# The running sum of a depthwise convolution: in one PSUM bank instead of SBUF

## The chip, the core and the metric

The kernel runs on one core of one Trainium2 chip. The metric is the device time of one launch in microseconds (us); lower is better. A measurement of this kernel can tell a difference of about 0.2%.

The engines are named as in the profile: PE is TensorE (matmuls; PEld is its weight load), DVE is VectorE, ACT is ScalarE, POOL is GpSimd, and SP is SyncE, whose queue issues nearly all DMAs. L506 is line 506 of the kernel. SBUF is the on-chip memory that all engines reach. PSUM holds eight banks of 128 partitions x 512 float32 values; matmuls write there.

## The reference, cut to what matters

Two residual layers of width 1024 over 512 positions. Layer 0 mixes positions with a Fourier half and a convolution half of 512 channels each, layer 1 with windowed attention, and each is followed by a mixture of 16 experts. The change lies in the convolution half of layer 0:

```python
def fourier_conv_mixer(h, w_in, conv_w, conv_b, ln_g, ln_b, w_out):
    proj = h @ w_in
    u_f = proj[..., :FOURIER_WIDTH]
    u_v = proj[..., FOURIER_WIDTH:FOURIER_WIDTH + CONV_WIDTH]
    u_g = proj[..., FOURIER_WIDTH + CONV_WIDTH:]
    ...
    glu = u_v * jax.nn.sigmoid(u_g)
    pad = CONV_KERNEL // 2
    conv = lax.conv_general_dilated(
        glu, conv_w[:, None, :], window_strides=(1,), padding=[(pad, pad)],
        dimension_numbers=("NWC", "WIO", "NWC"), feature_group_count=CONV_WIDTH) + conv_b
    y_c = jax.nn.silu(layer_norm(conv, ln_g, ln_b))
    return jnp.concatenate([y_f, y_c], axis=-1) @ w_out
```

The convolution is depthwise: each channel is filtered by itself, with 31 taps, over all 512 positions.

## The kernel before, in words

**Layout.** Activations lie transposed: channels on the 128 partitions, the 512 positions along the free dimension. The 512 convolution channels are four tiles, ct 0 to 3.

**The convolution.** `gated(ct)` multiplies the normalised input by the value and gate columns of `w_in` (three matmuls in `mm3`, L141 to L143, for one product in split precision) into two PSUM banks. `glu_of` then takes the sigmoid on ACT (L515) and writes the product to `glu[ct]` in SBUF on DVE (L516); in the trace that tile is named 3a for ct 0 and 1 and 3b for ct 2 and 3. `conv(ct, split)` sums 31 shifted copies of `glu[ct]`, each times one number per channel, into `ym[4 + ct]` (named 0b, SBUF). For ct 0, 2 and 3 all of it is DVE's: one `tensor_scalar` (L498) and thirty `scalar_tensor_tensor` (L506), each of which reads the shifted input and the sum from SBUF and writes the sum to SBUF. For ct 1 the argument is 30: ACT makes each tap's product (L503) in one of two buffers in 4b, and POOL adds it to the sum (L504).

**What else runs in that stretch.** PE does the projections, the Fourier half (`fourier`, `spectrum`: L542 to L544 and L551, with POOL additions L534 to L537 before them) and products that make the conditioning vectors (`ada_block`: L227, then L287, whose PSUM result DVE reduces at L289 and L290). Another way to the same kind of vector is `ada_steps`: DVE multiplies and adds weight tiles from DMA (L268, L266), or ACT and POOL do (L262, L264). Weights that need split precision go through `halves`: ACT rounds (L118), POOL or DVE subtracts (L119). `y_parts` does the same for an activation tile (L565 on ACT, L566 on POOL or DVE).

**After it.** Token L of the list `toks` needs all four tiles: it sums over channels with PE (`sums`, L579), forms the mean (L649) and subtracts it on DVE (L651). Token M does the same with squares (L656, L660, L666), token N normalises (L670, L671). The output projection (`out_mm`, `add_gated` L395), the router (L740 to L800) and the first mixture of experts (`moe`: L920 gathers tokens, L976 multiplies them by expert weights) follow.

**What sets the order.** `toks` gives the order in which the program is written. A scheduler with a timeline model then reorders the instructions of each engine, and each engine runs its own list strictly in order, waiting on semaphores. PSUM banks come from `free_banks`, eight in all, handed out and given back in the order of the code. Weight buffers (`Slot`, 11 of 1 MB and some areas lent to them) are handed out the same way, so a DMA into one waits until the buffer's last reader is done.

Of the kernel before, what the change touches and what calls it, by code (L numbers as in the profile page):

```python
# [12 lines left out]
AF = mybir.ActivationFunctionType  # L13
OP = mybir.AluOpType
# [18 lines left out]
def trunk(ctx: ExitStack, tc: tile.TileContext, x_d, c_d, pos_d, ada_w, ada_b, mix_g, ffn_g, w_in,  # L33
# [366 lines left out]
    def mixer0():  # L400
# [89 lines left out]

        def conv(ct, split):

            cv, g = ym[4 + ct], glu[ct]
            wt = lambda k: cw[:, 4 * k + ct:4 * k + ct + 1]
            if split:
                nc.scalar.activation(cv, g[:, 0:S], AF.Identity, scale=wt(0), bias=colsC[:, 24 + ct:25 + ct])
            else:
                nc.vector.tensor_scalar(cv, g[:, 0:S], wt(0), colsC[:, 24 + ct:25 + ct],  # L498
                                        op0=OP.mult, op1=OP.add)
            for k in range(1, TAPS):  # L500
                if k <= split:
                    f = taps[k % 2]
                    nc.scalar.activation(f, g[:, k:k + S], AF.Copy, scale=wt(k))  # L503
                    nc.gpsimd.tensor_add(cv, cv, f)  # L504
                else:
                    nc.vector.scalar_tensor_tensor(cv, g[:, k:k + S], wt(k), cv, op0=OP.mult, op1=OP.add)  # L506

        todo = [(0, 0, 4), (0, 0, 5)] + [(0, 1, j) for j in range(4)]
        G0 = None
        bs = [Bank() for _ in range(6)]  # L510
        pss = [b.__enter__() for b in bs]
        tiles = [(w, P * j) for j in range(2) for w in w0] + [(wf0, P * j) for j in range(2)]
        def glu_of(ct, pg, pv):
            sg = tmp()
            nc.scalar.activation(sg, pg, AF.Sigmoid)  # L515
            nc.vector.tensor_mul(glu[ct][:, PAD:PAD + S], pv, sg)  # L516

        def gated(ct):
            if ct > 1:
                bs_ = [Bank(), Bank()]  # L520
                ps = [b.__enter__() for b in bs_]
            else:
                bs_, ps = bs[2 * ct:2 * ct + 2], pss[2 * ct:2 * ct + 2]
            for p, m in zip(ps, w1 if ct > 1 else w0):
                proj(p, m, P * (ct % 2), range(0 if ct > 1 else 4, KT))
            glu_of(ct, *ps)
            back_banks(bs_)

        def spectrum(g, u):
# [68 lines left out]
        for tok in toks:  # L598
# [16 lines left out]
            elif op == 'n':  # L615
                lent = lend()
            elif op == 'F':
                us[j] = fourier(j)
            elif op == 's':
                G0 = G0 or Slot()  # L620
                if not ym[0]:
                    ym[0:4] = fourths("0a")
                spectrum(j, us.pop(j))
            elif op in "DE" and arg in ("d", "p"):
                drip += ada_steps(*(todo if op == 'D' else more)[j], arg == "p")
                if op == 'E':
                    more[j] = None
            elif op == 'D':
                ada_block(*todo[j], "0a" if arg else None)
            elif op == 'E':  # L630
                ada_block(*more[j])
                more[j] = None
            elif op == 'P':
                free_slots[:0] = [free_slots.pop(min(i, len(free_slots) - 1)) for i in picks]
            elif op == 'w':
                wf1 = wcols(256)
            elif op == 'H':
                G0.back()
                hh, hl = h_area()
                yp = list(zip(hh, hl))  # L640
                free_slots.extend(areas[2:])
            elif op == 'y':
                y_parts(j, eng)
            elif op == 'O':
                wo[j // 2, j % 2] = wo_half(j // 2, j % 2, eng)
            elif op == 'L':
                f = sums([ym[4 + ct] for ct in range(4)])
                with Bank() as pm:
                    nc.tensor.matmul(pm, mean4, f, start=True, stop=True)  # L649
                    for ct in range(4):  # L650
                        nc.vector.tensor_sub(ym[4 + ct], ym[4 + ct], pm)  # L651
                prefix_matrices()
            elif op == 'M':
                sq = [g[:, 0:S] for g in glu]
                for ct in range(4):
                    nc.scalar.activation(sq[ct], ym[4 + ct], AF.Square)  # L656
                f = sums(sq)
                with Bank() as pq:
                    for t in range(TT):
                        nc.tensor.matmul(pq[:, t:t + 1], f[:, P * t:P * t + P], ind, start=True, stop=True)  # L660
                    nc.vector.tensor_scalar(va, pq[:, 0:TT], 512 * EPS, None, op0=OP.add)
                rsqrt(rs, va, TT, 512 ** 0.5)
                prb = Bank()
                pr = prb.__enter__()
                for t in range(TT):
                    nc.tensor.matmul(pr[:, P * t:P * t + P], rs[:, t:t + 1].to_broadcast([P, P]), ident,  # L666
                                     start=True, stop=True)
            elif op == 'N':
                y = ym[4 + j]
                nc.vector.tensor_mul(y, y, pr)  # L670
                nc.scalar.activation(y, y, AF.Silu, scale=colsC[:, 28 + j:29 + j], bias=colsC[:, 32 + j:33 + j])  # L671
                y_parts(4 + j, nc.gpsimd if arg == 'g' else nc.vector)
                if j == 3:
                    prb.__exit__()
            elif op == 'e':
                early[j] = Bank()
                early[j] = early[j], early[j].__enter__()
                out_mm(early[j][1], j % TT, j // TT, range(4))
            elif op == 'B':
                row_bcast(gbc, mod[0, 0][:, 16:24])  # L680
            elif op == 'G':
                unlend(lent)
                free_slots.extend(areas[:2])
            elif op == 'T':
                rt = Router(0)
            elif op == 'm':
                first = 4
                if j not in early:
                    early[j] = Bank()
                    early[j] = early[j], early[j].__enter__()  # L690
                    first = 0
                t, hf = j % TT, j // TT
                out_mm(early[j][1], t, hf, range(first, KT))
                add_gated(t, hf, early[j][1], {'v': nc.vector, 'g': nc.gpsimd, None: nc.vector if hf else nc.gpsimd}[arg])
                early[j][0].__exit__()
                left[hf] -= 1
                if left[hf] == 0:
                    for i in range(2):
                        back(wo.pop((hf, i)))
            elif op == 'r':  # L700
                flip[0] = int(arg) if arg else flip[0]
                rt.part(j % 4, j // 4)
            elif op == 'V':
                drip += rt.early()
# [783 lines left out]
```

## Time and profile before

| | |
|---|---|
| Median of three runs | 1507.4 us (1506.88 to 1508.84) |
| The profiled execution, its own time | 1508.68 us |
| Its span, first to last instruction | 1507.0 us |
| Busy share of the span: PE, DVE, ACT, POOL | 91%, 42%, 22%, 21% |
| DMA | 480.69 MB, 319 GB/s on average |
| Mean granted TensorE clock | 0.961 |

The profile is one execution, so all sums below are made against its own 1508.68 us; 1.68 us of that lie around the span. Busy shares are averages over stages that have different limits, so a stage is read by itself, from a table of windows. In a timeline row the first number is the start and the second the time from there to the end of the last instruction that is merged into the row; instructions of one engine may overlap slightly, so the pace of a series is the distance from start to start.

### The profile page before, as it was taken

What the parts mean: (1) busy time and instruction counts of PE and PEld (TensorE: products, weight loads), DVE (VectorE), ACT (ScalarE), POOL (GpSimd) and SP (SyncE); (2) the same over time, 40 slices, a digit from 0 to 9 for tenths busy, and PEclk for the clock granted to TensorE, in tenths of its full rate; (3) what the DMA queues carried; (4) which work ended last, traced back from release to release, by engine and by line L of the source; (5) the groups of instructions that cost most, each with busy time, mean ns of one, the idle gap of its engine ahead of it and who ended that gap; (6) DMA issues with size and microseconds to landing.
All of it is one profiled execution on the core that took longest, in us unless ns stands there. A gap on an engine that the chain in (4) does not pass through costs nothing.

```text
span 1507.0 us, 18064 instructions
## 1 busy us (share of the span) xinstructions
PE 1367.3 (91%) x7203; PEld 764.9 (51%) x7203; DVE 635.7 (42%) x1165; ACT 337.7 (22%) x686; POOL 312.0 (21%) x234
## 2 busy tenths in 40 slices
PE   5994699899999999999878989989999999999996
PEld 3673475555355353453457656645554454443433
DVE  5599956322222221122267888771222222222114
ACT  3353343110010010100246554421110010010002
POOL 2587741200000000000046563500000000000002
PEclk8997899899999999999989999989999999999998
DMA  9466379789999999999910365877899999999995
GB/s 329 127 217 214 121 278 381 298 340 398 402 411 410 411 410 411 411 410 410 366 33 28 107 200 169 279 283 280 329 412 400 410 410 411 410 411 410 411 406 204
DMA packets 158428, 480.69 MB, mean 319 GB/s; under 512 B 10416, under 2 KB 31176, under 8 KB 158344
## 3 DMA queue, kind: packets, MB, share of 16 engines
q1 hardware_dynamic: 158264, 479.27, 83.0%
q8 instruction: 57, 0.93, 0.3%
q0 software_dynamic: 80, 0.26, 0.0%
q14 instruction: 27, 0.22, 0.0%
HBM read 477.40 MB, written 2.10 MB: 318 GB/s over the span
## 4 chain that ended last, share of the span: by engine, by line
PE 62%; DVE 17%; DMA 16%; ACT 2%; issue 1%; SPq 1%; POOL 0%; DVEq 0%; ACTq 0%; POOLq 0%
PE bank L976 32%; PE bank L920 8%; DVE 0b L506 7%; DMA w<-in_moe_w_up_dram 6%; DMA w<-in_moe_w_gate_dram 5%; PE bank L141 3%; PE bank L142 3%; PE bank L143 3%; PE bank L997 3%; PE bank L1014 3%; DMA 4b<-in_moe_w_gate_dram 2%; PE bank L227 2%; DMA 4a<-in_moe_w_up_dram 1%; PE bank L1305 1%; DMA 4a<-in_fc_w_in_dram 1%
## 5 line engine op out<-in xcount | busy, mean ns | idle before, releaser
L976 PE MATMUL bank<-w,area2b 128*64 128x512 f32 x744 | 194.3, 595 | 9.4 <-DMA w<-in_moe_w_gate_dram 6.5
L976 PE MATMUL bank<-w,area1b 128*64 128x512 f32 x688 | 182.0, 595 | 7.1 <-DMA w<-in_moe_w_up_dram 4.3
L976 PE MATMUL bank<-w,area1a 128*64 128x512 f32 x624 | 158.0, 593 | 3.4 <-ACT area1a L153 2.2
L1017 DVE TENSOR_TENSOR x<-x,bank 128x512 f32<-128x512 f32 (+1 forms) x136 | 78.8, 649 | 187.5 <-PE bank L1014 187.5
L909 POOL TENSOR_TENSOR tmp<-tmp,rr 128x512 f32<-128x512 f32 x14 | 17.7, 1265 | 589.6 <-DVE tmp L903 567.8
L976 PEld LDWEIGHTS bank<-w,area2b 128*64 128x64 f32 x744 | 62.0, 137 | 109.1 <-issue 85.4
L1067 DVE TENSOR_TENSOR area1a<-bank,area1a 128x512 f32<-128x512 f32 x32 | 22.1, 692 | 219.1 <-PE bank L976 219.1
L1007 DVE SCALAR_TENSOR_TENSOR tmp<-bank,af,gbc 128x512 f32<-128x512 f32 (+1 forms) x34 | 24.5, 720 | 213.3 <-PE bank L976 185.1
L976 PEld LDWEIGHTS bank<-w,area1b 128*64 128x64 f32 x688 | 58.8, 137 | 106.6 <-issue 84.6
L119 POOL TENSOR_TENSOR w<-w,w 128x1024 fp32r<-128x1024 f32 x30 | 75.5, 2533 | 148.6 <-ACT w L118 142.5
L976 PEld LDWEIGHTS bank<-w,area1a 128*64 128x64 f32 x624 | 53.1, 137 | 77.5 <-issue 70.1
L506 DVE SCALAR_TENSOR_TENSOR 0b<-3b,cw,0b 128x512 f32<-128x512 f32 x60 | 69.0, 1185 | 0.1
L1014 PE MATMUL bank<-area2a 128*128 128x512 f32 (+1 forms) x272 | 64.2, 386 | 5.1 <-ACT area2a L1008 5.1
L1008 ACT ACTIVATE area2a<-tmp 128x512 fp32r<-128x512 f32 (+1 forms) x34 | 20.6, 607 | 214.3 <-DVE tmp L1007 214.3
L1043 ACT ACTIVATE area1a<-bank 128x512 f32<-128x512 f32 x32 | 19.2, 599 | 195.4 <-PE bank L976 195.4
L1014 PEld LDWEIGHTS bank<-area2a 128*128 128x128 f32 x272 | 47.9, 188 | 28.2 <-ACT area1a L1043 9.7
L920 PE MATMUL bank<-tmp,0a 128*128 128x128 f32 x384 | 59.8, 278 | 0.0
L141 PE MATMUL bank<-area1a,w 128*128 128x512 f32 x132 | 53.0, 421 | 7.4 <-ACT area1a L377 6.6
L920 PE MATMUL bank<-tmp,0b 128*128 128x128 f32 x384 | 58.6, 275 | 0.0
L926 ACT ACTIVATE area1b<-bank,mod,a 128x128 f32<-128x128 f32 x32 | 14.6, 457 | 184.3 <-DVE area1b L928 184.3
L920 PEld LDWEIGHTS bank<-tmp,0a 128*128 128x128 f32 x384 | 50.5, 192 | 9.7 <-issue 9.7
L143 PE MATMUL bank<-area1a,w 128*128 128x512 f32 x132 | 53.4, 406 | 1.2 <-POOL w L119 1.2
(466 smaller groups left out, 2673.3 us busy)
## 6 DMA issues: line engine op xcount, KB each, us to landing
w<-in_moe_w_gate_dram SPq DMA_DIRECT2D x93, 1024.0 KB, 18.1
w<-in_moe_w_up_dram SPq DMA_DIRECT2D x86, 1024.0 KB, 18.2
w<-in_moe_w_down_dram SPq DMA_DIRECT2D x85, 1024.0 KB, 18.2
w<-in_ada_w_dram SPq DMA_DIRECT2D x44, 1024.0 KB, 7.0
3b<-in_moe_w_up_dram SPq DMA_DIRECT2D x10, 1024.0 KB, 18.6
4b<-in_moe_w_gate_dram SPq DMA_DIRECT2D x9, 1024.0 KB, 18.4
4a<-in_moe_w_gate_dram SPq DMA_DIRECT2D x9, 1024.0 KB, 18.0
3a<-in_moe_w_up_dram SPq DMA_DIRECT2D x9, 1024.0 KB, 15.5
```

What stands on the lines that cost most here:

```text
L119: eng.tensor_sub(lo.ap[:, s], w.ap[:, s], hi.ap[:, s].bitcast(FT))
L141: nc.tensor.matmul(ps, l[0], r[0], start=start, stop=False)
L142: nc.tensor.matmul(ps, l[0], r[1], start=False, stop=False)
L143: nc.tensor.matmul(ps, l[1], r[0], start=False, stop=stop)
L227: nc.tensor.matmul(ps[32 * q:32 * q + 32], cond[:, 4 * half + q], w[:, q], start=half == 0, stop=half == 1)
L506: nc.vector.scalar_tensor_tensor(cv, g[:, k:k + S], wt(k), cv, op0=OP.mult, op1=OP.add)
L920: nc.tensor.matmul(p[:, P * q:P * q + P], src_x(t, 4 * hf + q), oh[:, P * t:P * t + P], start=t == 0, stop=t == TT - 1)
L976: nc.tensor.matmul(ps[h][CAP * i:CAP * i + CAP], lhs[:, k, CAP * i:CAP * i + CAP], w[i].row(kk)[:, 512 * h:512 * h + 512], start=k == 0, s ...
L997: nc.tensor.matmul(ps[CAP * i:CAP * i + CAP, :n], lhs[:, k, CAP * i:CAP * i + CAP], w[i][:, kk], start=k == 0, stop=k == KT - 1)
L1007: nc.vector.scalar_tensor_tensor(f, ps[:, :n], af, gbc[:, s], op0=OP.mult, op1=OP.mult)
L1014: nc.tensor.matmul(p[:, :n], ohT[:, P * t:P * t + P], Y[z][:, c0:c0 + n], start=z == 0, stop=z == 1)
L1017: nc.vector.tensor_add(xx, xx, p[:, :n])
```

## The change

`conv` accumulates what DVE does of a channel tile in `acc`, a whole PSUM bank, and only the last tap of a tile writes to `ym[4 + ct]` in SBUF. The bank is one that ct 0's projection has used (`ps[1]`, bank_402 below): `gated(0)` no longer gives it back, and token L does, ahead of its first product. From there to token L the other users share seven banks. The ACT and POOL part (ct 1) is written anew and does what it did before.

```diff
         def conv(ct, split):
...
-            if split:
-                nc.scalar.activation(cv, g[:, 0:S], AF.Identity, scale=wt(0), bias=colsC[:, 24 + ct:25 + ct])
-            else:
-                nc.vector.tensor_scalar(cv, g[:, 0:S], wt(0), colsC[:, 24 + ct:25 + ct],
-                                        op0=OP.mult, op1=OP.add)
-            for k in range(1, TAPS):
-                if k <= split:
+                nc.scalar.activation(cv, g[:, 0:S], AF.Identity, scale=wt(0), bias=bias)
+                for k in range(1, split + 1):
                     f = taps[k % 2]
                     nc.scalar.activation(f, g[:, k:k + S], AF.Copy, scale=wt(k))
                     nc.gpsimd.tensor_add(cv, cv, f)
+            ks = range(split + 1 if split else 0, TAPS)
+            if not ks:
+                return
+            acc = sum_bank[1]
+            for k in ks:
+                out = cv if k == TAPS - 1 and not split else acc
+                if k == ks[0]:
+                    nc.vector.tensor_scalar(out, g[:, k:k + S], wt(k), None if split else bias, op0=OP.mult,
+                                            **({} if split else {"op1": OP.add}))
                 else:
-                    nc.vector.scalar_tensor_tensor(cv, g[:, k:k + S], wt(k), cv, op0=OP.mult, op1=OP.add)
+                    nc.vector.scalar_tensor_tensor(out, g[:, k:k + S], wt(k), acc, op0=OP.mult, op1=OP.add)
...
             glu_of(ct, *ps)
+            if ct == 0:
+                sum_bank.extend((bs_.pop(), ps[1]))
             back_banks(bs_)
...
             elif op == 'L':
+                sum_bank[0].__exit__()
                 f = sums([ym[4 + ct] for ct in range(4)])
```

The scheduler also moves instructions. The rows below are lists of instructions in the order in which an engine runs them: line, operation, output<-inputs with buffer numbers, size, and how many in a row. In the changed kernel a tap on DVE is L513, the first tap L510, the product of `glu_of` L528, and `y_parts` L580; the other names keep their lines up to L490.

First place: DVE from the first tap on. Before, the taps of two tiles alternate (3a is the input of ct 0, 3b of ct 2):

```order
L516 TENSOR_TENSOR 3a<-bank_402,tmp 128x512
L498 TENSOR_SCALAR 0b<-3a,cw,colsC 128x512
L506 SCALAR_TENSOR_TENSOR 0b<-3a,cw,0b 128x512 x7
L516 TENSOR_TENSOR 3a<-bank_404,tmp 128x512
L506 SCALAR_TENSOR_TENSOR 0b<-3a,cw,0b 128x512 x8
L516 TENSOR_TENSOR 3b<-bank_558,tmp 128x512
L506 SCALAR_TENSOR_TENSOR 0b<-3a,cw,0b 128x512
L498 TENSOR_SCALAR 0b<-3b,cw,colsC 128x512
L506 SCALAR_TENSOR_TENSOR 0b<-3a,cw,0b 128x512
L506 SCALAR_TENSOR_TENSOR 0b<-3b,cw,0b 128x512
```

Now one tile ends before the next begins, and the products of ct 2 and ct 3 (bank_558, bank_637) stand behind 15 and 30 taps of ct 0:

```order
L528 TENSOR_TENSOR 3a<-bank_402,tmp 128x512
L510 TENSOR_SCALAR bank_402<-3a,cw,colsC 128x512
L513 SCALAR_TENSOR_TENSOR bank_402<-3a,cw,bank_402 128x512 x7
L528 TENSOR_TENSOR 3a<-bank_404,tmp 128x512
L513 SCALAR_TENSOR_TENSOR bank_402<-3a,cw,bank_402 128x512 x8
L528 TENSOR_TENSOR 3b<-bank_558,tmp 128x512
L513 SCALAR_TENSOR_TENSOR bank_402<-3a,cw,bank_402 128x512 x14
L513 SCALAR_TENSOR_TENSOR 0b<-3a,cw,bank_402 128x512
L528 TENSOR_TENSOR 3b<-bank_637,tmp 128x512
L510 TENSOR_SCALAR bank_402<-3b,cw,colsC 128x512
L513 SCALAR_TENSOR_TENSOR bank_402<-3b,cw,bank_402 128x512 x14
L289 TENSOR_REDUCE mod_107<-bank_704 128x4
```

What moved: each tap now has the tap before it as its input, with none of another tile between them, and the product from bank_637 comes ahead of all taps of 3b.

Second place: the end of the convolution on DVE. Before, the weight split (L119) and the steps on a weight tile from DMA (w_1386, L268 and L266) stand behind the last tap:

```order
L506 SCALAR_TENSOR_TENSOR 0b<-3b,cw,0b 128x512
L290 TENSOR_TENSOR mod_108<-mod_108,colsA 128x4
L119 TENSOR_TENSOR w_1188<-w_1185,w_1187 128x1024 x2
L268 TENSOR_SCALAR w_1386<-w_1386,sil 128x512
L266 SCALAR_TENSOR_TENSOR w_1386<-w_1386,sil 128x512 x3
L651 TENSOR_TENSOR 0b<-0b,bank_1052 128x512 x4
```

Now they, and the steps on the next tile (w_1467), stand between the last taps (from the row of w_1386 on):

```order
L268 TENSOR_SCALAR w_1386<-w_1386,sil 128x512
L513 SCALAR_TENSOR_TENSOR bank_402<-3b,cw,bank_402 128x512
L266 SCALAR_TENSOR_TENSOR w_1386<-w_1386,sil 128x512
...
L266 SCALAR_TENSOR_TENSOR w_1467<-w_1467,sil,w_1386 128x512
L513 SCALAR_TENSOR_TENSOR bank_402<-3b,cw,bank_402 128x512
...
L266 SCALAR_TENSOR_TENSOR w_1467<-w_1467,sil 128x512
L513 SCALAR_TENSOR_TENSOR bank_402<-3b,cw,bank_402 128x512 x5
L513 SCALAR_TENSOR_TENSOR 0b<-3b,cw,bank_402 128x512
L666 TENSOR_TENSOR 0b<-0b,bank_1052 128x512 x4
```

What moved: two L119, one L268 and seven L266 went ahead of the last tap. The last 13 taps stand behind the DMA that fills w_1386, and the last nine behind the one that fills w_1467.

Third place: PE between the last tile's channel sum and the mean (L579 and L649 before, L593 and L664 now). Before, 18 products of the output projection (L141 to L143) stood there; now there are three small ones:

```order
L593 MATMUL bank_1046<-0b,one 32x512 x2
L556 MATMUL bank_1115<-4a,3b 128x256
L557 MATMUL bank_1115<-4a,3b 128x256
L558 MATMUL bank_1115<-4a,3b 128x256
L664 MATMUL bank_1052<-tmp,mean_96 128x512
```

What moved: those output products went ahead of the last channel sum.

## Rows read from the trace of the kernel before

**Rows 1.** The chain that ended last, by line (the page's fourth part).

```profile
PE bank L976 32%; PE bank L920 8%; DVE 0b L506 7%; DMA w<-in_moe_w_up_dram 6%; DMA w<-in_moe_w_gate_dram 5%; PE bank L141 3%; PE bank L142 3%; PE bank L143 3%; PE bank L997 3%; PE bank L1014 3%; DMA 4b<-in_moe_w_gate_dram 2%; PE bank L227 2%; DMA 4a<-in_moe_w_up_dram 1%; PE bank L1305 1%; DMA 4a<-in_fc_w_in_dram 1%
```

**Rows 2.** Windows: busy us of each engine, granted clock, DMA share, GB/s.

```profile
core 0: us, PE busy (x) PEld busy (x) DVE busy (x) ACT busy (x) POOL busy (x), PEclk, DMA share, GB/s
69.30:184.60 115.30, 82.79 (x402) 58.41 (x400) 114.65 (x113) 45.52 (x66) 91.03 (x54) 0.85 0.50 173
...
264.00:290.00 26.00, 20.88 (x128) 15.26 (x126) 9.61 (x40) 1.65 (x4) 6.34 (x7) 0.80 0.64 247
330.00:700.00 370.00, 356.60 (x1868) 171.57 (x1866) 83.41 (x145) 33.73 (x64) 7.82 (x6) 1.00 1.02 409
```

**Rows 3.** Groups by shape on DVE: count, busy us, mean ns, idle before.

```profile
L506 DVE SCALAR_TENSOR_TENSOR 0b<-3b,cw,0b 128x512 f32<-128x512 f32 x60 | 69.0, 1185 | 0.1
L506 DVE SCALAR_TENSOR_TENSOR 0b<-3a,cw,0b 128x512 f32<-128x512 f32 x30 | 41.5, 1384 | 0.5
```

**Rows 4.** Timeline of DVE: start, us, instruction; from 88 us.

```profile
89.67 0.68 DVE L516 TENSOR_TENSOR 3b<-bank,tmp 128x512 f32<-128x512 f32 x1
...
94.49 1.78 DVE L506 SCALAR_TENSOR_TENSOR 0b<-3b,cw,0b 128x512 f32<-128x512 f32 x1
```

**Rows 5.** Timeline of POOL, the same stretch.

```profile
87.46 9.95 POOL L504 TENSOR_TENSOR 0b<-0b,4b 128x512 f32<-128x512 f32 x6
```

**Rows 6.** Timeline of DVE while POOL has no add.

```profile
143.11 0.16 DVE L289 TENSOR_REDUCE mod<-bank 128x4 f32<-128x16 f32 x1
143.20 1.40 DVE L506 SCALAR_TENSOR_TENSOR 0b<-3b,cw,0b 128x512 f32<-128x512 f32 x2
...
144.59 10.67 DVE L506 SCALAR_TENSOR_TENSOR 0b<-3b,cw,0b 128x512 f32<-128x512 f32 x16
```

**Rows 7.** Line L376 on DVE: ns min/median/max, first and last start.

```profile
L376 DVE SCALAR_TENSOR_TENSOR 0a<-0a,a,w x4: 745/746/752, 767.8 to 771.4; 128x512 f32<-128x512 f32 x4
L376 DVE SCALAR_TENSOR_TENSOR 0b<-bank,a,w x4: 737/742/747, 772.7 to 779.6; 128x512 f32<-128x512 f32 x4
```

**Rows 8.** Timeline of DVE: the first tap; two taps of one sum.

```profile
69.31 0.55 DVE L498 TENSOR_SCALAR 0b<-3a,cw,colsC 128x512 f32<-128x512 f32 x1
...
179.74 1.54 DVE L506 SCALAR_TENSOR_TENSOR 0b<-3b,cw,0b 128x512 f32<-128x512 f32 x2
```

**Rows 9.** Timeline of POOL: a spectrum's four adds, then the first taps.

```profile
71.23 0.79 POOL L534 TENSOR_TENSOR 3a<-tmp 128x256 f32<-128x256 f32 x1 [9.09 <-ACT tmp L560]
...
74.00 0.90 POOL L537 TENSOR_TENSOR 3a<-3a 128x128 f32<-128x128 f32 x1
78.39 3.54 POOL L504 TENSOR_TENSOR 0b<-0b,4b 128x512 f32<-128x512 f32 x2 [3.48 <-ACT 4b L503]
```

**Rows 10.** Lines L264 and L119 on POOL: ns min/median/max, first and last start.

```profile
L264 POOL TENSOR_TENSOR w<-w x6: 1287/1294/1627, 213.1 to 222.3; 128x512 f32<-128x512 f32 x6
...
L119 POOL TENSOR_TENSOR 4b<-w,4a x2: 2400/2620/2841, 194.8 to 197.1; 128x1024 fp32r<-128x1024 f32 x2
```

**Rows 11.** Waits of SP's queue, 69 to 250 us: total, times, longest.

```profile
SPq L103 <- POOL w L119: 21.5, 1, 21.5
```

**Rows 12.** DMA issues from 69 to 185 us: count, size, median to landing.

```profile
w<-in_ada_w_dram SPq DMA_DIRECT2D x15, 1024.0 KB, 5.3
```

**Rows 13.** Timeline of DVE behind the last tap.

```profile
184.57 2.35 DVE L119 TENSOR_TENSOR w<-w,w 128x1024 fp32r<-128x1024 f32 x2
...
187.36 2.33 DVE L266 SCALAR_TENSOR_TENSOR w<-w,sil 128x512 f32<-128x512 f32 x3
```

**Rows 14.** Timeline of PE from the last channel sum to the mean.

```profile
184.64 1.04 PE L579 MATMUL bank<-0b,one 128*32 128x512 f32 x2 [0.16 <-DVE 0b L506]
...
189.83 1.02 PE L649 MATMUL bank<-tmp,mean 128*128 128x512 f32 x2
```

**Rows 15.** Waits from 69 to 250 us: total, times, longest.

```profile
PE bank L542 <- DVE 3b L516: 9.9, 1, 9.9
...
PE bank L551 <- DVE mod L289: 9.9, 1, 9.9
```

More of the change, by code (lines that the diff above doesn't have):

```diff
@@ L494, in conv @@
             wt = lambda k: cw[:, 4 * k + ct:4 * k + ct + 1]
+            bias = colsC[:, 24 + ct:25 + ct]
             if split:
-                nc.scalar.activation(cv, g[:, 0:S], AF.Identity, scale=wt(0), bias=colsC[:, 24 + ct:25 + ct])
-            else:
-                nc.vector.tensor_scalar(cv, g[:, 0:S], wt(0), colsC[:, 24 + ct:25 + ct],
-                                        op0=OP.mult, op1=OP.add)
-            for k in range(1, TAPS):
-                if k <= split:
+                nc.scalar.activation(cv, g[:, 0:S], AF.Identity, scale=wt(0), bias=bias)
+                for k in range(1, split + 1):
                     f = taps[k % 2]
@@ L504, in conv @@
                     nc.gpsimd.tensor_add(cv, cv, f)
-                else:
-                    nc.vector.scalar_tensor_tensor(cv, g[:, k:k + S], wt(k), cv, op0=OP.mult, op1=OP.add)
+            ks = range(split + 1 if split else 0, TAPS)
[7 more added lines that the diff above has]
+                                            **({} if split else {"op1": OP.add}))
+                else:
+                    nc.vector.scalar_tensor_tensor(out, g[:, k:k + S], wt(k), acc, op0=OP.mult, op1=OP.add)
+            if split:
+                nc.vector.tensor_add(cv, acc, cv)
         todo = [(0, 0, 4), (0, 0, 5)] + [(0, 1, j) for j in range(4)]
@@ L512, in mixer0 @@
         tiles = [(w, P * j) for j in range(2) for w in w0] + [(wf0, P * j) for j in range(2)]
+        sum_bank = []
         def glu_of(ct, pg, pv):
```

## The prediction

> **What bounds the kernel now.** I read the chain that ended last first. The taps on DVE, L506, hold 7% of it [rows 1], about 105 us, and no other DVE line is named. They form one stretch, from the first tap at 69.31 us to the last one's end at 184.6. The windows say who works there: DVE 114.65 of 115.30 us, POOL 91.03, PE 82.79, DMA at half of its capacity [rows 2]. So DVE sets the pace, and what a tap costs decides.
>
> The groups by shape show that 90 taps of one and the same shape cost 1185 and 1384 ns on average, 110.5 us in all [rows 3]. The timelines show why. While POOL adds without a pause (six adds in 9.95 us) [rows 5], a tap takes 1.78 us; while it has none, sixteen taps take 10.67 us, 0.66 from start to start [rows 6]. Beside POOL's adds stands an instruction that is not stretched: the product of the gates, at 89.67, takes 0.68 [rows 4]. It reads one operand from a bank and one from SBUF and writes SBUF. A tap of before reads two tensors from SBUF. So what makes DVE and POOL wait for each other is, by these rows, the second SBUF input, and the change takes exactly that away: a tap now reads its input from SBUF and the sum from PSUM.
>
> **A tap.** What a bank as input costs is shown: the same operation takes 742 ns with one input from a bank, 746 with both from SBUF [rows 7]. No row shows DVE writing to PSUM. Below I bound a tap by 0.68, the shortest row of this size with a bank [rows 4]; above by 1.78, the longest that is typical now [rows 4]. I take the nearest, two taps of one sum that follow each other with POOL silent: 1.54 for both, less 0.75 for the second, so 0.79 from start to start [rows 8]. That is more than 0.66 because each waits for the one before, and in the new order all do.
>
> [...]
>
> **DVE's own sum.** From 69.3: 90 taps x 0.79 = 71.1; three first taps of 0.55 [rows 8] and 0.03 to the next, 1.7; three more products of 0.68 [rows 4], 2.0; fifteen small instructions on the conditioning vectors, 0.1 each from start to start (143.11 to 143.20) [rows 6], 1.5, and one activation split, 0.7. The order also moved work ahead of the last tap: two L119 in 2.35, and L268 with seven L266, each 0.75 at most (three take 2.33) [rows 13], 8.4 together. The end would be 69.3 + 71.1 + 1.7 + 2.0 + 2.2 + 8.4 = 154.7. What moved is not new work; before, it stood behind the last tap, beside PE's products.
>
> **What the moved work waits for.** L268 now stands ahead of 13 taps, and its weight tile comes by a DMA that SP could not issue until POOL had split an older tile: 21.5 us of SP's waiting ended with POOL's L119 [rows 11]. So POOL's list becomes the second bound. It starts its taps of ct 1 at 78.39 [rows 9]. A lone add of this size takes 1.29 [rows 10], and I take 1.37 with the hand-over to the next; 30 of them are 41.1. Four L119 up to that split, 2.4 each [rows 10], are 9.6. One activation split is 1.4. Three spectra of four small adds took 3.67 each beside DVE's taps (71.23 to 74.90) [rows 9]; I let them shrink by a fifth, as an add does from 1.66 (9.95 by six) [rows 5] to 1.37, to 8.8 in all. That gives 78.4 + 41.1 + 9.6 + 1.4 + 8.8 = 139.3. The DMA lands 5.3 later [rows 12], at 144.6.
>
> DVE alone would stand at L268 at 154.7 - 13 x 0.79 - 8 x 0.75 = 138.4. It waits 6.2 us, with 13 taps behind it. The next tile follows after one more activation split and two L119: 139.3 + 1.4 + 4.8 + 5.3 = 150.8. DVE gets there from 144.6 by four steps of 0.75 and four taps, 6.2 us, at the same 150.8. Then four steps and nine taps, 10.1: **the last tap ends at 160.9**, 23.7 us earlier than at 184.6. A tap may cost up to 0.87 (0.79 + 6.2 by the 77 taps ahead of L268) before this end moves much; up to that price POOL and the DMA set it, not DVE.
>
> **Behind it.** PE took from 184.64 to 189.83 from the last channel sum to the mean [rows 14]: 1.04 for the sum and 4.15 in which 18 output products stood in its list. Those now stand ahead; three small products and ACT's copy of the sums remain, for which I leave 1.0. That gains 3.1. It could be nothing, if PE has not done the 18 in time, and 4.15 at most.
>
> The taps on ACT and POOL are the same instructions, and ACT's cost nothing here: it is busy 45.52 of 115.30 us [rows 2]. The bank that is kept costs nothing while PE finds another; the rivals price it. All later work keeps its order but for details, and moves as a whole: between 264 and 290 us the DMA engines are busy 0.64 [rows 2], so the stream of expert weights waits for buffers there, and its start is PE's to set.
>
> Sum: 23.7 + 3.1 = 26.8 us. The profiled execution took 1508.7, 1.3 more than the median of the runs shown, so 1508.7 - 26.8 = 1481.9. I forecast **1482 us**. The forecast's own range: no wait for the moved loads gives 154.7 in place of 160.9, 1476, and where a step and a tap alternate at 0.66 instead of up to 0.79 another 2 us; a tap at 0.87, or nothing gained behind, gives 1485 to 1488.
>
> **Rivals.**
>
> *One bank too few.* PE waited 9.9 us for a bank that DVE's late product held, and 9.9 for one that a late reduction held [rows 15]. With seven banks one such wait may remain, and POOL's spectra with it. POOL's list, the loads and the last tap then come 9.9 later, 170.8: a gain of 13.8 + 3.1, **1492**. Against it: both readers now come early in DVE's list. Chance 0.14.
>
> *A dear write.* A tap at 1.0 ends DVE's sum at 154.7 + 90 x 0.21 = 173.6, past the loads: a gain of 11.0 + 3.1, **1495**; at 1.1 it is 1504. For it speaks that each tap waits for a write to PSUM to be read again, which no row shows. Chance 0.10 for 0.95 to 1.15.
>
> *Slower: the tap is not relieved.* If the stretch comes from any SBUF access, and not from the second input, the chain of taps goes on alternating with POOL at the 1.23 it averages now (110.5 by 90) [rows 3]. DVE's sum then ends at 154.7 + 90 x 0.44 = 194.3, since the moved work is ahead of it; with 3.1 back behind it the kernel is 6.6 us slower, **1515**. The point from which it decides is a tap of 1.16 (154.7 + 33 by 90 over 0.79). The upper bound of 1.78 would make 1565. This is also the case in which the change does not do what it says. Against it stands the product at 89.67 [rows 4], and the 1.28 us or so that POOL needs alone. Chance 0.06, slower.
>
> *Eaten later.* Between 330 and 700 us the DMA engines are full, 1.02 [rows 2]. If the stream of weights starts only half as much earlier, since its own loads stand behind others that now come closer together, 13.4 remain: **1495**. Against it speaks the 0.64 ahead of that stretch. Chance 0.08.
>
> The forecast has 0.62. What 0.2%, 3 us, or more faster would be (the least that a measurement of this kernel can tell) holds for the forecast, the first and the last rival and nearly all of the second: 0.91. Slower by that: 0.06. Between: 0.03, a tap near 1.16. The range from 1473 to 1499 takes in the forecast with its bounds, the first and last rival, and the second up to a tap of 1.05; left out are the slower case and the rest of the second.
>
> **What would show it.** Right: L513 at 0.7 to 0.8 us with POOL's adds beside it; POOL's adds at 1.3; L268 of the first weight tile waiting for a DMA, with taps behind it; the last tap near 161 and the mean 2 us later. Wrong: taps over 0.9 with POOL silent (the write), taps that are long only beside POOL (not relieved), PE or POOL waiting some 10 us for a bank before 150 us, or a gain at the mean that is gone by 700 us.

## The result, and the profile after

The changed kernel takes **1488.9 us** (median of four, 1486.9 to 1489.9) against 1507.2 (1506.9 to 1508.8) for the kernel before on the same chip: ratio **0.9875** (95% interval 0.9858 to 0.9892), 18.3 us less. The forecast was 1482 with a range from 1473 to 1499. Its gain of 26.8 us was counted from the profiled 1508.7; between the profiled executions 20.1 came, between the medians 18.3. The profiled execution took 1488.62 us, its span is 1486.8.

The chain that ended last, by line, of the changed kernel; against [rows 1] the taps fall from 7% to 1%:

```profile
PE bank L991 32%; PE bank L935 8%; DMA w<-in_moe_w_up_dram 6%; DMA w<-in_moe_w_gate_dram 5%; PE bank L141 4%; PE bank L142 4%; PE bank L143 4%; PE bank L1012 3%; PE bank L1029 3%; DMA 4b<-in_moe_w_gate_dram 2%; PE bank L1320 1%; DVE bank L513 1%; PE bank L227 1%; PE bank L1286 1%; DMA 4a<-in_moe_w_up_dram 1%; PE bank L1311 1%
```

The groups by shape on DVE (count, busy us, mean ns, idle before), for [rows 3]:

```profile
L513 DVE SCALAR_TENSOR_TENSOR bank<-3b,cw,bank 128x512 f32<-128x512 f32 x58 | 43.7, 754 | 1.3
L513 DVE SCALAR_TENSOR_TENSOR bank<-3a,cw,bank 128x512 f32<-128x512 f32 x29 | 21.9, 755 | 1.0
```

The timeline of POOL in the same stretch, for [rows 5] and [rows 9]:

```profile
71.11 0.46 POOL L550 TENSOR_TENSOR 3a<-3a 128x128 f32<-128x128 f32 x1
...
92.71 13.60 POOL L502 TENSOR_TENSOR 0b<-0b,4b 128x512 f32<-128x512 f32 x10 [0.18 <-ACT 4b L501]
```

A tap is 0.75 us, beside POOL's adds or not, where it was 1.19 and 1.38 on average; ten adds of POOL take 13.60 us, where six took 9.95.

Windows of the changed kernel: first tap to last tap, then to the router's first product (L771, L756 before); and below it the second stretch of the kernel before, which [rows 2] does not have:

```profile
67.80:162.40 94.60, 78.13 (x411) 55.61 (x409) 84.54 (x122) 47.39 (x69) 63.63 (x54) 0.94 0.70 245
162.40:214.20 51.80, 49.99 (x226) 37.43 (x227) 20.79 (x36) 17.91 (x28) 18.76 (x14) 0.97 0.56 203
```

```profile
184.60:235.70 51.10, 51.06 (x235) 38.80 (x236) 30.55 (x47) 19.78 (x31) 18.02 (x14) 1.00 0.82 298
```

The stretch of the taps shrinks from 115.3 to 94.6 us. All that follows keeps its length within 1.3 us. The table divides each profiled execution at the same instructions; PE's idle time is the length of the two middle stretches less PE's busy time in them.

| us | to first tap | first to last tap | to the router | rest | PE busy, idle in both |
|---|---|---|---|---|---|
| before | 69.3 | 115.3 | 51.1 | 1271.3 | 133.9, 32.5 |
| changed | 67.8 | 94.6 | 51.8 | 1272.6 | 128.1, 18.3 |
| e1 sum in SBUF | 67.3 | 125.1 | 47.8 | 1269.9 | 134.2, 38.7 |
| e2 bank held only | 67.3 | 116.5 | 56.2 | 1269.6 | 134.5, 38.2 |
| e5 ten taps less | 67.7 | 83.2 | 47.4 | 1271.1 | 125.4, 5.2 |
| e6 two banks | 68.4 | 76.4 | 51.6 | 1272.1 | 124.6, 3.4 |
| e9 two banks, ten less | 68.4 | 71.3 | 60.4 | 1270.5 | 126.3, 5.4 |
| e10 second bank held | 68.6 | 94.4 | 52.0 | 1269.4 | 126.1, 20.3 |

The first column (67.3 to 69.3) and the rest (1269.4 to 1272.6) vary without a pattern that these runs show; what a version is worth is read from the two middle stretches.

### The profile page after: what moved, and what is told of

Its sections match the earlier page's. It is cut to its first block, busy times and chain, and to the rows that moved or that the text cites. A ratio compares the mean times of both kernels' runs of the same rounds, so it can differ in the third digit from the quotient of the medians.

```text
span 1486.8 us, 18062 instructions
## 1 busy us (share of the span) xinstructions
PE 1363.0 (92%) x7203; PEld 762.8 (51%) x7203; DVE 595.5 (40%) x1165; ACT 336.3 (23%) x685; POOL 285.9 (19%) x234
## 4 chain that ended last, share of the span: by engine, by line
PE 67%; DMA 17%; DVE 11%; ACT 3%; issue 1%; SPq 1%; POOL 0%; DVEq 0%; ACTq 0%
PE bank L991 32%; PE bank L935 8%; DMA w<-in_moe_w_up_dram 6%; DMA w<-in_moe_w_gate_dram 5%; PE bank L141 4%; PE bank L142 4%; PE bank L143 4%; PE bank L1012 3%; PE bank L1029 3%; DMA 4b<-in_moe_w_gate_dram 2%; PE bank L1320 1%; DVE bank L513 1%; PE bank L227 1%; PE bank L1286 1%; DMA 4a<-in_moe_w_up_dram 1%; PE bank L1311 1%
## 5 line engine op out<-in xcount | busy, mean ns | idle before, releaser
L119 POOL TENSOR_TENSOR w<-w,w 128x1024 fp32r<-128x1024 f32 x30 | 73.1, 2455 | 147.7 <-ACT w L118 144.6
L1029 PEld LDWEIGHTS bank<-area2a 128*128 128x128 f32 x272 | 47.8, 188 | 30.4 <-ACT area1a L1058 9.7
L141 PE MATMUL bank<-area1a,w 128*128 128x512 f32 x132 | 53.1, 421 | 6.0 <-ACT area1a L377 3.9
L143 PE MATMUL bank<-area1a,w 128*128 128x512 f32 x132 | 53.2, 406 | 1.3 <-POOL w L119 1.3
L142 PE MATMUL bank<-area2a,w 128*128 128x512 f32 x132 | 53.2, 404 | 0.1
## 6 DMA issues: line engine op xcount, KB each, us to landing
4a<-in_moe_w_gate_dram SPq DMA_DIRECT2D x9, 1024.0 KB, 18.3
```

The costliest lines, as they stand in the source:

```text
L119: eng.tensor_sub(lo.ap[:, s], w.ap[:, s], hi.ap[:, s].bitcast(FT))
L141: nc.tensor.matmul(ps, l[0], r[0], start=start, stop=False)
L142: nc.tensor.matmul(ps, l[0], r[1], start=False, stop=False)
L143: nc.tensor.matmul(ps, l[1], r[0], start=False, stop=stop)
L1029: nc.tensor.matmul(p[:, :n], ohT[:, P * t:P * t + P], Y[z][:, c0:c0 + n], start=z == 0, stop=z == 1)
```

## The experiments

**e1: the same list, the sum in SBUF.**

```diff
-            acc = sum_bank[1]
+            acc = gbc[:, 0:S]
```

> The changed kernel with its running sum in a tile of SBUF that has 512 unused values until the gate rows are written (gbc), the bank still held: POOL's list is the same word for word and DVE's differs by single places, so that nearly only the memory of the sum differs. Theory (two SBUF inputs are what makes DVE and POOL wait for each other): a tap takes 1.2 us or more on average, up to 1.8 beside POOL's adds, and 0.75 with POOL silent; POOL's adds take 1.6 again in place of 1.3. 90 taps at 1.2 to 1.3 instead of 0.78 put the last tap 30 us or more behind that of the changed kernel (162.3), near 190 to 200, later than before the change, since eight weight steps now stand ahead of it: 1512 to 1525 us. Rival (the gain comes from the new order, one tile after the other, and not from PSUM): taps stay near 0.8, the last one near 162, 1487 to 1492 us.

Measured: 1511.5 us, ratio 1.0036 (1.0025 to 1.0048), half a microsecond below the theory's range; the last tap ends at 192.4, inside it. The groups by shape on DVE:

```profile
L513 DVE SCALAR_TENSOR_TENSOR gbc<-3b,cw,gbc 128x512 f32<-128x512 f32 x58 | 64.4, 1111 | 1.3
L513 DVE SCALAR_TENSOR_TENSOR gbc<-3a,cw,gbc 128x512 f32<-128x512 f32 x29 | 41.7, 1436 | 1.0
```

and POOL's adds (ns min/median/max):

```profile
L502 POOL TENSOR_TENSOR 0b<-0b,4b x30: 1437/1622/1852, 76.4 to 153.5; 128x512 f32<-128x512 f32 x30
```

With nearly the same list on all engines, the memory of the sum is worth the whole difference: the last tap comes 125.1 us after the first instead of 94.6, and the kernel is 5.5 us slower than before the change. The order alone gains nothing; it loses, with the moved work ahead of a late last tap.

**e2: the bank alone.**

```diff
-            acc = sum_bank[1]
+            acc = cv
```

> The kernel before, with one bank kept from the first product to token L and not used: seven banks for the others, the sum in SBUF in the tile's own place, the taps of two tiles alternating as before. Theory: the bank is worth little, 1504 to 1511 us, and the whole gain of the change comes from the tap. Rival (fewer banks move PE's and DVE's order, and that by itself gains or loses): over 5 us off 1507, with a wait of some 10 us for a bank, on PE, where it loses, or with the output products ahead of the last channel sum and 1 to 3 us less where it gains.

Measured: 1512.5 us, ratio 1.0042 (1.0027 to 1.0056). The theory's 1504 to 1511 was too low: one bank costs 6.5 us here. Waits of PE, 67 to 250 us (total, times, longest), and the window from the last tap to the router:

```profile
PE bank L556 <- DVE mod L289: 20.7, 2, 19.2
```

```profile
183.80:240.00 56.20, 54.40 (x241) 40.89 (x242) 32.62 (x48) 19.77 (x31) 18.81 (x14) 0.96 0.65 225
```

That is the rival's mechanism, and that of the prediction's "one bank too few": PE waits 19.2 us for the bank that a late reduction holds, where it was 9.9 [rows 15]. DVE, the bound, is not held by it (116.5 us against 115.3), but PE has more left to do behind the last tap, 56.2 us against 51.1.

**e3: the sum alternates between SBUF and the bank.**

```diff
-            acc = sum_bank[1]
+            both = (sum_bank[1], cv)
...
-                out = cv if k == TAPS - 1 and not split else acc
+                out, acc = both[(k + 1) % 2], both[k % 2]
```

> Odd taps read the sum from SBUF and write it to the bank, even taps read it from the bank and write it to SBUF; each tap touches SBUF twice and PSUM once. Theory (the second SBUF input decides): the taps that write the bank take 1.2 us or more on average and up to 1.8, those that read the bank 0.75 throughout; the time lies about half way, 1495 to 1507 us. Rival 1 (the number of SBUF accesses, reads and writes alike): both kinds are stretched alike, near 1.1. Rival 2 (PSUM on either side is enough): both at 0.75, and the time is that of the changed kernel, 1486 to 1492 us.

Measured: 1492.2 us in one run. The groups by shape on DVE, the timelines of DVE and POOL:

```profile
L513 DVE SCALAR_TENSOR_TENSOR bank<-3b,cw,0b 128x512 f32<-128x512 f32 x30 | 31.7, 1057 | 0.7
L513 DVE SCALAR_TENSOR_TENSOR 0b<-3b,cw,bank 128x512 f32<-128x512 f32 x30 | 22.4, 745 | 0.6
L513 DVE SCALAR_TENSOR_TENSOR bank<-3a,cw,0b 128x512 f32<-128x512 f32 x15 | 15.1, 1009 | 0.5
L513 DVE SCALAR_TENSOR_TENSOR 0b<-3a,cw,bank 128x512 f32<-128x512 f32 x15 | 11.2, 746 | 0.5
```

```profile
88.96 0.87 DVE L513 SCALAR_TENSOR_TENSOR bank<-3a,cw,0b 128x512 f32<-128x512 f32 x1
89.86 0.75 DVE L513 SCALAR_TENSOR_TENSOR 0b<-3a,cw,bank 128x512 f32<-128x512 f32 x1
90.64 0.89 DVE L513 SCALAR_TENSOR_TENSOR bank<-3a,cw,0b 128x512 f32<-128x512 f32 x1
```

```profile
85.97 11.82 POOL L502 TENSOR_TENSOR 0b<-0b,4b 128x512 f32<-128x512 f32 x7
```

This separates input from output. Taps that read two tensors from SBUF are stretched though they write PSUM (1.04 us on average, 46.8 by 45); taps that read the bank are not, though they write SBUF (0.75, longest 0.751). So the second SBUF input of a tap decides; the count of accesses and the write don't. The size was missed: 1.04, not 1.2 or more, and the time is 3 us below the range, where rival 2 had put it (1486 to 1492); so the rows of the taps decide here and not the time. They also show why: a pair of taps takes 1.68 us (88.96 to 90.64) beside one add of POOL (11.82 by 7, 1.69). Before, one tap (1.78 [rows 4]) stood beside one add (1.66 [rows 5]). As the times fit together, and that is an estimate from them, POOL's add runs while DVE makes the tap that reads the bank (0.75), and the next tap (0.87 here) finds POOL nearly done.

**e4: before, without POOL's adds.**

```diff
-                    nc.gpsimd.tensor_add(cv, cv, f)
+                    if k == 1:
+                        nc.gpsimd.tensor_add(cv, cv, f)
```

> The kernel before, with 29 of the 30 adds of the second channel tile on POOL left out (so that tile's sum lacks 29 taps). Theory (DVE's taps are long only because POOL adds beside them): taps with both inputs in SBUF fall to 0.66 to 0.8 us, 90 of them take about 65 us from start to start in place of 110, and the last one ends between 145 and 155 instead of at 184.6; 1475 to 1482 us. Rival (a tap on SBUF is long by itself, for instance since it reads what the one before has just written): taps stay at 1.2 to 1.4 us on average, the time within 5 us of 1507.

Measured: 1483.2 us in one run; the taps (L507 here; ns min/median/max, first and last start):

```profile
L507 DVE SCALAR_TENSOR_TENSOR 0b<-3b,cw,0b x60: 733/752/2926, 89.5 to 155.5; 128x512 f32<-128x512 f32 x60
L507 DVE SCALAR_TENSOR_TENSOR 0b<-3a,cw,0b x30: 740/752/2779, 69.1 to 107.7; 128x512 f32<-128x512 f32 x30
```

A tap in SBUF is 0.75 too when POOL adds nothing beside it; the long ones that remain lie beside what POOL has left, the spectra and the weight splits. The last tap ends at 156.2 and the time is 1483, each 1 us past the range given. Taking the adds away does to DVE what the bank does.

**e5: ten taps less.**

```diff
-            ks = range(split + 1 if split else 0, TAPS)
+            ks = [k for k in range(split + 1 if split else 0, TAPS) if ct != 2 or k not in range(10, 20)]
```

> The changed kernel without ten of the 31 taps of channel tile 2 (taps 10 to 19), which is the last tile in DVE's list. Theory (DVE's own list sets the last tap, and PE, which waited 12.2 us for it in the changed kernel, passes all of it on): ten taps at 0.79 us and four weight steps that now stand behind the last tap, less some 2 us for the weight tile whose load was issued at 136.8: the last tap ends near 153 to 154 instead of 162.3, the mean 8 to 9 us earlier, 1479 to 1482 us. Rival (POOL's list and the loads behind it set the end, as the prediction had it): DVE waits for the first or second moved weight tile, the last tap ends no earlier than 158, 1485 to 1489 us. Second rival (PE's own backlog sets the end): last tap early, but the router's first product no more than 4 us earlier than at 214.2.

Measured: 1471.2 us in one run, 8 us below what any theory gave. The timeline of DVE:

```profile
147.10 0.48 DVE L268 TENSOR_SCALAR w<-w,sil 128x512 f32<-128x512 f32 x1
...
150.14 0.74 DVE L513 SCALAR_TENSOR_TENSOR 0b<-3b,cw,bank 128x512 f32<-128x512 f32 x1
```

The last tap ends at 150.9, 11.4 us earlier than in the changed kernel, and no moved step waits for a DMA: DVE's own list sets the end, not POOL's. The end of the kernel moves by 17.4 us (spans), more than the last tap. Of the other 6, 4.4 lie between the last tap and the router, and 1.5 in the rest, which is within what that column varies by. Rows of the changed kernel, and below them the stretch behind the last tap in e5:

```profile
162.38 1.92 PE L593 MATMUL bank<-0b,one 128*32 128x512 f32 x4 [12.22 <-DVE 0b L513]
```

```profile
162.40:164.30 1.90, 1.90 (x5) 0.24 (x5) 0.00 (x0) 0.00 (x0) 0.00 (x0) 0.50 0.00 0
```

```profile
150.90:198.30 47.40, 47.36 (x227) 36.76 (x228) 22.31 (x41) 20.20 (x32) 18.04 (x14) 1.00 0.70 250
```

After 12.2 us without work PE runs at a granted clock of 0.50 behind the last tap. In e5 PE waits 1.7 us and keeps 1.00. From the last tap to the router it needs 47.4 us, not 51.8: 2.6 less of PE's busy time (47.4 against 49.99), and 1.8 in which PE of the changed kernel waits for ACT. That the long wait is what brings the low clock isn't shown: in e6, after a wait of 2.0 us, the three small products behind the channel sum (145.79 to 148.63) take 1.14, 1.06 and 1.06 us, where they take 0.70, 0.59 and 0.59 in e5.

**e6: two banks.** Tile 2 gets a sum of its own in the other bank of the first product.

```diff
-                sum_bank.extend((bs_.pop(), ps[1]))
-            back_banks(bs_)
+                sum_bank.extend((list(bs_), ps))
+            back_banks([] if ct == 0 else bs_)
...
-            acc = sum_bank[1]
+            acc = sum_bank[1][ct == 2]
...
-                sum_bank[0].__exit__()
+                back_banks(sum_bank[0])
```

> Both banks of the first product are kept, and channel tile 2 has its own sum in the second one, so the scheduler alternates taps of two tiles again; six banks remain. Theory (a tap follows one of another sum at 0.66 us from start to start, one of its own at 0.79): about 70 of the 90 taps at 0.66 gain some 9 us, the waits of DVE of 2.9 and 3.4 us go in part, and the weight steps stand behind the last tap again (5 us): the last tap between 146 and 152 us, and as PE waited 12.2 us for it, 1477 to 1482 us. Rival (the second lost bank costs more than that, as one bank did in the list of before, where it took 6.5 us): PE waits 10 us or more for a bank before the last tap, 1486 to 1495 us.

Measured: **1469.2 us**, ratio 0.9756 (0.9742 to 0.9771); it leaves nothing out and beats both kernels. The theory's 1477 to 1482 was 8 us too high, and its last tap (146 to 152) too late: it ends at 144.8. Windows to the last tap and on to the router:

```profile
68.40:144.80 76.40, 73.00 (x399) 52.18 (x397) 72.22 (x112) 44.47 (x65) 63.70 (x54) 1.00 0.74 263
144.80:196.40 51.60, 51.58 (x236) 40.00 (x237) 30.12 (x47) 20.63 (x32) 18.74 (x14) 0.97 0.73 264
```

Most taps follow one of another sum and start 0.66 us after it; the weight steps are behind the last tap again. PE is idle for 3.4 us in both stretches together.

**e7: eight taps to ACT and POOL.** In the list of tokens:

```diff
-c2.0
+c2.8
```

> Eight taps of channel tile 2 go to ACT and POOL (POOL was idle for 24.7 us ahead of the mean), DVE does the other 23 products and adds the two parts. DVE: 8 taps of 0.79 less, one addition of 0.7 more, four weight steps now behind the last tap (2.6): its list ends near 154 us instead of 162.3. POOL: its convolution work ended at 142.7; eight adds of 1.3 end at 153. Theory: last tap 153 to 156 us, 1480 to 1484 us. Rival (POOL's two adds ahead of its weight splits delay the load for DVE's moved steps, or POOL's chain of ACT products is slower than 1.3 a tap): last tap after 159 us, 1486 to 1492 us.

Measured: 1486.2 us, ratio 0.9867 (0.9850 to 0.9884), not to be told from the changed kernel. The timelines of POOL and DVE:

```profile
140.11 4.76 POOL L119 TENSOR_TENSOR w<-w,w 128x1024 fp32r<-128x1024 f32 x2
144.84 7.54 POOL L502 TENSOR_TENSOR 0b<-0b,4b 128x512 f32<-128x512 f32 x4
```

```profile
142.54 3.42 DVE L119 TENSOR_TENSOR w<-w,w 128x1024 fp32r<-128x1024 f32 x1
...
156.28 0.75 DVE L266 SCALAR_TENSOR_TENSOR w<-w,sil,w 128x512 f32<-128x512 f32 x1 [1.36 <-DMA w<-in_ada_w_dram]
157.07 4.11 DVE L266 SCALAR_TENSOR_TENSOR w<-w,sil 128x512 f32<-128x512 f32 x3
```

The rival's time came, with DVE's list at its end only at 161.8, but mostly by another mechanism than the rival's, that of the taps of before: of the work that DVE has left there, L119 and L266 read two SBUF tensors. The first split takes 3.42 us instead of 1.22. It starts at 142.54 and meets POOL's own weight splits, which end at 144.87; in the changed kernel DVE came to it at 145.05, and POOL's splits, with no new adds ahead of them, had ended at 142.68. Beside POOL's adds the second split takes 1.65, L268 1.48 instead of 0.48, and the last three L266 4.11 instead of 2.33. With two L266 of 1.09 instead of 0.74 that is 6.1 us in all. Of what the rival named, DVE's wait for a load is there, with 1.36 us. What eight taps gave was taken back.

**e8: the weight steps to ACT and POOL.**

```diff
-E3.d:04
+E3.p:04
```

> The eight weight steps that the change moved ahead of the last tap on DVE (L268 and seven L266) are done by ACT and POOL instead, in the 24.7 us in which POOL waited for the mean. Theory (DVE's list sets the last tap): eight steps of 0.66 less, seven taps back from 0.66 to 0.79: last tap near 158 instead of 162.3, 1483 to 1486 us. Rival (ACT's part, which waits for the DMA, holds up ACT's sums or squares, or POOL's seven adds of 1.3 end too late for what needs the vector): last tap early, but the mean or the normalised tiles no earlier, 1487 to 1492 us.

Measured: 1484.3 us, ratio 0.9851 (0.9835 to 0.9868), as the theory had it, but the interval overlaps the changed kernel's, so that a gain over it isn't shown. The timelines of DVE and POOL:

```profile
149.03 9.45 DVE L513 SCALAR_TENSOR_TENSOR bank<-3b,cw,bank 128x512 f32<-128x512 f32 x12
158.51 0.75 DVE L513 SCALAR_TENSOR_TENSOR 0b<-3b,cw,bank 128x512 f32<-128x512 f32 x1
```

```profile
150.32 3.95 POOL L264 TENSOR_TENSOR w<-w 128x512 f32<-128x512 f32 x3
```

Twelve taps now run in one row, at 0.79, the first seven of them beside POOL's adds of weight steps; they take no harm from them. The last tap ends at 159.3.

**e9: e6 with ten taps less.** The edit is that of e5.

> The version with two sums in two banks, and ten taps of channel tile 2 left out as in the run with ten taps less. In the version with two banks PE was busy 72.8 of the 76.2 us up to the last tap and waited only 2.0 us for it. Theory (PE's own work is the next bound): DVE's taps end 6 to 7 us earlier, near 138, and the time moves by no more than 3 us: 1465 to 1470 us, with no row in which PE waits for a tap. Rival (DVE's taps set the end still): the time falls with the last tap, 1460 to 1463 us.

Measured: 1472.3 us in one run, 2 us above the theory's range. The last tap ends 5 us earlier than in e6, at 139.7, and the kernel gains nothing; the window behind it:

```profile
139.70:200.10 60.40, 57.67 (x254) 43.43 (x255) 35.49 (x52) 22.29 (x34) 21.69 (x16) 0.97 0.71 256
```

PE's own work is the next bound: what the taps give back stands behind the last tap as PE's backlog, 60.4 us instead of 51.6.

**e10: a second bank held.** As e6, with all sums in one of the two banks:

```diff
-            acc = sum_bank[1][ct == 2]
+            acc = sum_bank[1][1]
```

> The changed kernel with both banks of the first product kept, but all sums in one of them, one after the other: six banks for the others, and no taps that alternate. Theory (in the new order DVE reads its banks early, so a bank less makes nobody wait, and the gain of two sums comes from their alternating): within 3 us of the changed kernel, 1486 to 1492 us. Rival 1 (a bank costs some 6 us, as in the order of before): 1493 to 1498 us. Rival 2 (the gain of the version with two banks came from what the scheduler makes of six banks): 1469 to 1480 us.

Measured: 1484.9 us, ratio 0.9861 (0.9841 to 0.9882), not to be told from the changed kernel's 0.9875, and 1 us below the theory's range. With one more bank held, in the new order, PE waits 15.3 us for the last tap and for nothing else longer than 2.0. So neither the second bank nor the order that comes with it makes e6 fast; it owes its gain to the taps that alternate.

## Why the forecast was right, and where its sizes were off

**A tap: right.** Forecast 0.79 from start to start in a chain; measured 0.79, and 0.66 between steps of other work. Of the bounds 0.68 and 1.78 the row nearest to the new order, two taps of one sum with nothing of POOL beside them, was the one to take. The write to PSUM costs a tap nothing that shows: 0.754 us, against a median of 0.752 in SBUF without POOL's adds (e4). The upper end of the forecast's own range was set too high: by the prediction's own sums a tap at 0.87 gives 1483 (13 taps of 0.08 more behind the load), nothing gained behind 1485, and both 1486, not 1488.

**POOL's list: right.** The split that gates the load was forecast to end at 139.3, counted from a first tap at 69.3; it ended at 136.8 with the first tap at 67.8, 1 us early. An add takes 1.29. In part this is luck: POOL waited 3.7 us for ACT within that stretch, which the sum left out, and the three spectra came to 6.7 us instead of 8.8 and the adds to 39.4 instead of 41.1.

**"POOL and the DMA set it, not DVE": wrong.** This is the step that failed. DVE reached L268 after the load, and waited for nothing there. The timelines of POOL, of SP and of DVE:

```profile
132.06 4.72 POOL L119 TENSOR_TENSOR w<-w,w 128x1024 fp32r<-128x1024 f32 x2
```

```profile
136.80 17.34 SPq L103 DMA_DIRECT2D w<-in_ada_w_dram  x5
```

```profile
67.80 0.81 DVE L510 TENSOR_SCALAR bank<-3a,cw,colsC 128x512 f32<-128x512 f32 x1
...
96.87 0.69 DVE L528 TENSOR_TENSOR 3b<-bank,tmp 128x512 f32<-128x512 f32 x1 [2.85 <-PE bank L143]
97.60 0.81 DVE L510 TENSOR_SCALAR bank<-3b,cw,colsC 128x512 f32<-128x512 f32 x1
...
124.78 0.69 DVE L580 TENSOR_TENSOR area2a<-0a,area1a 128x512 fp32r<-128x512 f32 x1 [3.41 <-ACT area1a L579]
...
138.62 1.75 DVE L322 SCALAR_TENSOR_TENSOR a<-mod,colsC 128x4 f32<-128x4 f32 x1
...
140.95 1.87 DVE L753 TENSOR_TENSOR aw<-rw,a 128x128 f32<-128x128 f32 x1
...
147.98 0.48 DVE L268 TENSOR_SCALAR w<-w,sil 128x512 f32<-128x512 f32 x1
```

From the first tap to L268 the sum had 69.1 us (138.4 less 69.3); it took 80.2 (147.98 less 67.80). The 11.1 us are waits of 7.6 that the sum left out (2.85 for the product of tile 3, 3.41 for ACT's rounding of an activation tile, two shorter ones of 0.59 and 0.74), some 4.8 by which seven small instructions with two SBUF inputs were stretched beside POOL (L322 and L753 alone 1.6 and 1.7 over the 0.1 forecast for each), and 0.7 for three first taps of 0.7 to 0.85 in place of 0.58, less 2.1 for some 16 taps at 0.66. The prediction held for the taps that a second SBUF input makes DVE wait, and then priced the small instructions as if it didn't. Behind L268 it took 14.3 us and not the forecast 22.5: the 6.2 of waiting are gone, as the loads were there, and 2.0 more, as taps and steps that alternate start every 0.66. So two wrong terms nearly cancel, which is luck: the last tap ends 94.5 us after the first, forecast 91.6, before 115.3. e5 shows which of them bounds: ten taps less, and it came 11.4 us earlier.

**"Behind it, 3.1": gone.** The mean came 4.95 us after the last tap (162.32 to 167.27) and not 6.27; that gains 1.3. Of the other 1.8 an estimated 1.5 went with the low clock (0.50): the same steps take 3.46 us in e5 (150.88 to 154.34), where the clock is 1.00. By the router it is -0.7 (51.8 against 51.1): with output products moved ahead PE has only 1.1 us less to do there (49.99 against 51.06), and it waits 1.8 for ACT.

**"All later work moves as a whole": right** within 1.3 us (1271.3 and 1272.6), which is less than the versions differ there by themselves. The sum as measured is 20.8 for the taps less 0.7 and 1.3, 18.8 us, close to the 18.3 of the medians; the spans differ by 20.2, since the profiled execution of before started its taps 1.5 later.

**The rivals.** *One bank too few* exists (e2: 19.2 us of PE's waiting, 6.5 us of the kernel) where DVE reads the banks late; e10, with two held and DVE early, has no loss. *A dear write*: not for a tap, but for the first tap of each tile, 0.81 us instead of 0.55. *Not relieved*: excluded by the taps, and e1 shows what the case would have cost, 1511.5 us where it was priced at 1515. *Eaten later*: the rest is unchanged.

What stays open: whether a better place for the one instruction at 124.78 would be worth the 3.41 us that DVE waits for ACT there, in the version with one bank. ACT had waited 1.73 us for the load of an output weight, until 118.88, and then worked through its list without a pause up to that rounding at 124.12. A better place wasn't tried, since in e6 PE is full there.

## What to carry to other kernels

Where DVE and POOL work beside each other for long, look for DVE instructions with two SBUF inputs: here one operand in PSUM took DVE out of POOL's way (a tap from 1.19 and 1.38 us on average to 0.75), and a bank that nobody missed paid for it. If the instructions form a chain, give two chains a bank each, so that each starts 0.66 us after another instead of 0.79 after its own (e6). Then count the idle time of the engine behind (PE: 32.5, 18.3, 3.4 us), which says how much more there is to get, and leave POOL's idle time alone if DVE's work beside it has two SBUF inputs: in e7 eight taps given to POOL brought nothing that could be told (1486.2 us against 1488.9).

## What the runs showed of the hardware that was not expected

*POOL was shut out for long.* In [rows 6] sixteen taps of before run at 0.66 us, and the prediction, and the heading of those rows, read that as a stretch in which POOL has no add. The timeline of POOL in the kernel before says otherwise:

```profile
147.55 8.63 POOL L536 TENSOR_TENSOR 3b<-3b 128x128 f32<-128x128 f32 x1 [10.88 <-PE bank L542]
```

An addition that takes 0.46 us in the changed kernel (71.11, above) took 8.63: it ended at 156.18, behind the last of the sixteen at 155.26. So while those taps followed each other at 0.66, POOL's add was not done. The same is in e2 (ns min/median/max) and in e4:

```profile
L502 POOL TENSOR_TENSOR 0b<-0b,4b x30: 1263/1622/9354, 76.4 to 161.7; 128x512 f32<-128x512 f32 x30
```

```profile
106.51 9.20 POOL L535 TENSOR_TENSOR 3a<-tmp 128x256 f32<-128x256 f32 x1 [21.47 <-ACT tmp L561]
```

Two things come together in all three: the taps of two sums run at 0.66, and POOL comes back from 10.88, 11.69 and 21.47 us without work. Neither by itself did it in these runs. Taps of two sums alternate in the kernel before from 92.79 to 114.86 too, beside a POOL that adds without a pause, and there each took 1.78 and POOL's adds came through at 1.66 [rows 4, rows 5]. In e1 POOL came back from 6.96 us without work to a single chain, and none of its adds lasted over 1.85. Why the two together shut POOL out is not shown.

*One tap in two was free.* In e3 DVE did two taps in 1.68 us beside POOL's adds, where one of before took 1.78 [rows 4]: only the one with two SBUF inputs was stretched (1.04 on average, the other 0.75).

*The first tap was dearer in PSUM, and not stretched there.* A `tensor_scalar` from SBUF to SBUF took 0.55 us alone [rows 8], but 1.51 in the kernel before beside POOL's adds (at 91.36), and in e3, beside POOL's adds, 1.34 to 1.38, with one SBUF input only (ns min/median/max):

```profile
L510 DVE TENSOR_SCALAR 0b<-3b,cw,colsC x2: 1343/1364/1384, 83.4 to 98.1; 128x512 f32<-128x512 f32 x2
```

To a bank it took 0.81, beside POOL's adds too (97.60, above). The prediction had missed both, the higher price in PSUM (0.81 against 0.55) and the stretching in SBUF (up to 1.51): a second SBUF input is not the only thing that makes DVE wait for POOL. What the other is, these runs don't show.
